# Up projections of m-tiles 2 and 3 as seven block products

## The chip, the cores and the metric

One core of one Trainium2 chip runs the kernel. The metric is the device time of one execution in microseconds (us); three runs of the kernel before took 2712.07 to 2712.29 us, median 2712.2.

## What is computed

A decoder trunk of two layers on one sequence of 512 tokens, 1024 wide, in f32. A layer is a feed-forward half-step (`ffn1`), a mixer with two branches, and a second feed-forward half-step (`ffn2`). Each sub-layer normalizes x and modulates it by a conditioning vector c. Cut to the part that the change touches:

```python
D_MODEL = 1024; SEQ = 512; DEPTH = 2; D_FF = 2816
def swiglu(h, w1, w3, w2):
    return (jax.nn.silu(h @ w1) * (h @ w3)) @ w2
# for each layer:
mod = cond @ ada_w[l] + ada_b[l]
sh1, sc1, g1, sh2, sc2, g2, sh3, sc3, g3 = jnp.split(mod, N_MOD, axis=-1)
h = modulate(x, norm_ffn1[l], sh1, sc1)
x = x + 0.5 * (1.0 + g1)[:, None] * swiglu(h, ffn1_w1[l], ffn1_w3[l], ffn1_w2[l])
...
h = modulate(x, norm_ffn2[l], sh3, sc3)
x = x + 0.5 * (1.0 + g3)[:, None] * swiglu(h, ffn2_w1[l], ffn2_w3[l], ffn2_w2[l])
```

## The kernel before

Activations lie with the feature on the partitions: eight tiles of 128 features by 512 tokens. TensorE (PE) works in a 32-bit format that is short of f32, so every operand is split in a high and a low part: ScalarE (ACT) casts the high part, VectorE (DVE) subtracts it from the value for the low part, and a product is three matmuls: high by high, high by low, low by high (`mm3`, L129). `hhi` and `hlo` are the two parts of h.

A feed-forward's 2816 hidden features are 22 m-tiles of 128. An up projection of one m-tile by w1 or w3 loads a slab of 128x1024 weights (512 KB, `slab`, L115), splits it in two halves of 512 and runs 8 x 3 matmuls of 512 columns. There are two ways in which an m-tile's hidden features come about:

- plain: `first` (L546) does m-tiles 0 and 1 from slabs, three of them loaded and split during the sub-layer before (`early`); `up` (L535) does one more m-tile from two slabs. `glu` (L529) makes silu(p1) * p3 and splits it.
- pairs (`pairs`, L630): two m-tiles at once. The 1024 inputs are halved in two blocks of 512, the two m-tiles are the two block columns, the 512 tokens are halved in two. Of the 2x2 by 2x2 product of blocks, seven products are made instead of eight, with sums of weight blocks and combinations of h's blocks (a scheme of Strassen's kind). One product is 24 matmuls of 256 columns and does w1 and w3 together. The seven weight forms (`weights`, L599) are a11, f1, f1+a11, a12, f3, a12+f2 and a22: f1 and f3 are sums of two blocks made on the way in by a load and an accumulating load that POOL issues (`block_sum`, L577), two are made by DVE, and each form is cast by ACT and subtracted by DVE as one piece of 128x1024 (L604 and L605). h's four combinations (`fast_acts`, L470) are made from f32 copies of h, kept in eight "quarters" in the buffers `c3` and `cv`: DVE subtracts (L496) and makes `minus_sum` (L493), POOL subtracts two (L498), ACT and DVE split each into the buffers `A` (L488, L489). They come in four parts, one for each `next(make)`.

The very first feed-forward starts from `first_begun`, with m-tiles 0 to 5 plain. The other three run `first`, two `up`s (m-tiles 2 and 3), pairs from 4 to 9, the first third of the down projection, pairs 10 to 17, the second third, pairs 18 to 21, and the last third (`close`, L422). `early_sums` starts the two sums of the next pairs ahead. `tick` takes the next entry of a queue of `ada_block`s (L276): each loads 512 KB of conditioning weights in an `L` buffer and is one DVE multiplication with a sum (L281). The gate that the first down projection needs is the first eight entries.

Buffers are rings: `raw` has 2, `whi` and `wlo` 3 each, `L` 5, `A` 2; PSUM has `acc` 3, `sc` 2, `sm` 2, `po` 1. Each engine runs its instructions in a fixed order that was set when the program was built; those wrapped in `ordered` keep their order in the text, the others are placed by the builder's scheduler. SP issues most loads, in one queue; POOL issues the accumulating ones, in its own.

Of the kernel before, what the change touches and what calls it, by code (L numbers as in the profile page):

```python
# [73 lines left out]
class Trunk:  # L74
# [435 lines left out]
    def ffn(self, l, w, gate, finish, early, ahead=None):  # L510
# [6 lines left out]
        def up_slab(src, m):  # L517
            return self.slab(src[l, m].rearrange("p k c -> p (k c)"), 1024)

        def place(m):  # L520
            if m in (8, 9):
                hi, lo = (self.t("c3", [P, SEQ], F32R) for _ in range(2))
            else:
                o = self.t("O", [P, 2, SEQ], F32R)
                hi, lo = o[:, 0, :], o[:, 1, :]
            g[m] = (hi, lo)
            return hi, lo

        def glu(m, ps1, ps3):  # L529
            s = self.t("g", [P, SEQ])  # L530
            nc.scalar.activation(s, ps1, AF.Silu)
            nc.vector.tensor_mul(s, s, ps3)
            self.split(*place(m), s)

        def up(m, make):  # L535
            s1 = up_slab(w1, m)
            s3 = up_slab(w3, m)
            next(make)
            ps1, ps3 = self.p("acc"), self.p("sc")
            self.proj(ps1, s1, acts)  # L540
            self.proj(ps3, s3, acts)
            glu(m, ps1, ps3)
            if m > 1:
                self.tick(2)

        def first():  # L546
            s10, s30, s11 = early
            p10, p30, p11 = self.p("acc"), self.p("sc"), self.p("acc")
            for cols in HALVES:
                for k in range(KT):  # L550
                    for s, p in ((s10, p10), (s30, p30), (s11, p11)):
                        self.proj(p, s, acts, cols, (k,))
            glu(0, p10, p30)
            s31 = self.slab(w3[l, 1].rearrange("p k c -> p (k c)"), 1024,
                            tuple(self.t("O", [P, 1024], F32R) for _ in range(2)))
            p31 = self.p("sc")
            self.proj(p31, s31, acts)
            glu(1, p11, p31)
            return 2

        def first_begun():
            n = len(early) // 2
            s = up_slab(w3, n)
            for m in range(n):
                glu(m, early[2 * m], early[2 * m + 1])
            ps = self.p("sc")
            self.proj(ps, s, acts)
            glu(n, early[2 * n], ps)
            return n + 1
# [12 lines left out]
        def loads(m, sums_first=False):  # L582

            st = {}
            st["f1"] = block_sum(m + 1, 0, m + 1, 1)
            if sums_first:
                st["f3"] = block_sum(m + 1, 0, m, 0)
            yield st
            st["a11"] = block("raw", m, 0)
            yield st  # L590
            if not sums_first:
                st["f3"] = block_sum(m + 1, 0, m, 0)
                yield st
            st["a12"] = block("raw", m, 1)
            yield st
            st["a22"] = block("L", m + 1, 1)
            yield st
# [29 lines left out]
                    self.mm(ps[:, i, :], f[0][:, c], x[1], start=False, stop=False, skip_group_check=True)  # L627
                    self.mm(ps[:, i, :], f[1][:, c], x[0], start=False, stop=k == 3, skip_group_check=True)

        def pairs(ms, comb, lds, make=iter(())):  # L630
            half = lambda tag: self.t(tag, [P, 2, 256])
            bank = lambda tag: self.p(tag, [P, 2, 256])
            stream, steps = [], iter(())
# [14 lines left out]
            for m in ms:  # L648
# [13 lines left out]
                for step in range(7):  # L662
# [36 lines left out]
                    else:  # L699
# [1 line left out]
                        s = self.t("cv", [P, 256])  # L701
                        gated(x, 1, HALVES[0], s)
                        self.split(*place(m + 1), gm[1])
                self.tick(2)

        def early_sums(m):
            lds = loads(m, True)
            next(lds)
            return lds
# [12 lines left out]
                       (0, 0) if i == 2 else (2, 1), 4 if i == 2 else 0)  # L722

        begun = len(early) > 3
        plain = 6 if begun else 4
        m = first_begun() if begun else first()
        comb = []
        make = self.fast_acts(comb)
        lds = early_sums(plain)
        while m < plain:  # L730
            up(m, make)
            m += 1
        pairs(range(plain, 10, 2), comb, lds, make)
        lds = early_sums(10)
        down(0)
        pairs(range(10, 18, 2), comb, lds)
        lds = early_sums(18)
        down(1)
        pairs(range(18, FT, 2), comb, lds)
        down(2)  # L740

# [969 lines left out]
```

## Time and profile before

| | |
|---|---|
| median of three runs | 2712.2 us (2712.07 to 2712.29) |
| the profiled execution's own time | 2711.74 us |
| its span, first to last instruction | 2709.6 us |
| PE busy | 2678.9 us (99%) |
| DVE busy | 1988.0 us (73%) |
| ACT busy | 1283.3 us (47%) |
| POOL busy | 225.8 us (8%) |
| granted TensorE clock | 1.00 |

The span is 2.1 us shorter than the time of its execution. Times below are counted from the span's start. In a row of the order of time stand: start, length, engine, line, operation, out<-in by the program's names, shape, and in brackets how long the engine had been idle and who ended that. In a row of a stretch stand: the stretch, its length, then each engine's busy time and number of instructions, the clock, the DMA share and GB/s. PEld is the weight load beside a matmul. q1 is SP's DMA queue and q0 POOL's.

The second feed-forward of layer 0 has its opening products from 1018.0 to 1036.86, the fourth projection and both `up`s to 1064.64, and three pairs to 1125.12.

### The profile page before, as it was taken

Reading aid. Unit: us, or ns where it says so; the run is one execution under the profiler, and the core shown is the slowest. Engines: PE = TensorE matmul, PEld = TensorE weight load, DVE = VectorE, ACT = ScalarE, POOL = GpSimd, SP = SyncE. Lnnn points to the kernel's source line nnn. Section 1 sums busy time; section 2 is a strip of 40 time slices with the busy share of each in tenths; the row PEclk is TensorE's granted clock in tenths of the full one; section 3 lists DMA queues with packets and bytes.
Section 4 is the critical chain, followed back from the end, with each engine's and each line's share of the span. In section 5 each row is a group of like instructions: output and inputs, shape, how many; then the busy total and the mean of one; then the engine's idle time right before and its main releaser. Section 6 shows DMA issues by size and latency. Waiting matters only on the chain.

```text
span 2709.6 us, 44272 instructions
## 1 busy us (share of the span) xinstructions
PE 2678.9 (99%) x17028; PEld 2380.4 (88%) x17028; DVE 1988.0 (73%) x4129; ACT 1283.3 (47%) x2549; POOL 225.8 (8%) x368
## 2 busy tenths in 40 slices
PE   7999999999999999999999999999999999999999
PEld 6989997888888789999999999888888888998988
DVE  6877868777668777785677877786777687685745
ACT  4535355544446436443554344545444564453533
POOL 0000012000001011000010000120000111110000
PEclk9999999999999999999999999999999999999999
DMA  9678723222122563785528875232222225456642
GB/s 308 183 233 225 230 90 118 90 69 84 64 80 72 170 203 113 241 239 154 154 84 227 244 241 162 95 119 76 82 81 73 73 84 183 156 166 177 168 130 85
DMA packets 119107, 394.64 MB, mean 146 GB/s; under 512 B 13552, under 2 KB 16368, under 8 KB 118896
## 3 DMA queue, kind: packets, MB, share of 16 engines
q1 hardware_dynamic: 106368, 350.39, 39.1%
q0 software_dynamic: 10080, 36.70, 7.6%
q10 hardware_dynamic: 2448, 4.72, 0.5%
q8 instruction: 134, 2.20, 0.3%
q14 instruction: 77, 0.63, 0.1%
HBM read 376.55 MB, written 15.20 MB: 145 GB/s over the span
## 4 chain that ended last, share of the span: by engine, by line
PE 94%; DVE 2%; ACT 2%; DMA 0%; issue 0%; POOL 0%; SPq 0%; ACTq 0%; DVEq 0%
PE acc L95 67%; PE sc L95 18%; PE sm L95 6%; PE sm L100 2%; PE po L95 1%; ACT whi L123 0%; ACT g L1274 0%; DVE wlo L124 0%; PE po L100 0%; DMA M<-in_x 0%; DMA raw<-in_w_in 0%; DVE A L1234 0%; DVE mx L1269 0%; DVE s L1229 0%; ACT hhi L401 0%
## 5 line engine op out<-in xcount | busy, mean ns | idle before, releaser
L123 ACT CAST whi<-raw 128x512 fp32r<-128x512 f32 (+2 forms) x548 | 315.5, 607 | 444.0 <-PE acc L95 216.2
L95 PE MATMUL acc<-hhi,whi 128*128 128x512 f32 (+1 forms) x1368 | 505.5, 370 | 2.3 <-ACT whi L1527 2.3
L95 PE MATMUL acc<-hhi,wlo 128*128 128x512 f32 (+1 forms) x1368 | 487.3, 356 | 0.0
L95 PE MATMUL acc<-hlo,whi 128*128 128x512 f32 (+1 forms) x1368 | 485.4, 355 | 0.0
L124 DVE TENSOR_TENSOR wlo<-raw,whi 128x512 fp32r<-128x512 f32 (+2 forms) x548 | 374.8, 703 | 122.6 <-ACT whi L123 115.6
L95 PE MATMUL acc<-O,whi 128*128 128x512 f32 x1472 | 454.7, 390 | 0.0
L95 PE MATMUL acc<-A,whi 128*128 128x256 f32 (+1 forms) x1808 | 346.5, 291 | 0.3 <-ACT g L684 0.2
L95 PEld LDWEIGHTS acc<-O,whi 128*128 128x128 f32 x1472 | 274.9, 188 | 56.2
L95 PEld LDWEIGHTS acc<-hhi,wlo 128*128 128x128 f32 x1368 | 259.2, 189 | 38.6 <-DVE wlo L124 1.9
L95 PEld LDWEIGHTS acc<-A,whi 128*128 128x128 f32 x1808 | 286.1, 192 | 5.7 <-ACT g L684 0.4
L95 PE MATMUL acc<-O,wlo 128*128 128x512 f32 x736 | 286.8, 390 | 0.0
L95 PEld LDWEIGHTS acc<-hhi,whi 128*128 128x128 f32 x1368 | 259.9, 190 | 30.3 <-ACT whi L1527 2.4
L95 PEld LDWEIGHTS acc<-hlo,whi 128*128 128x128 f32 x1368 | 260.2, 190 | 27.1
L95 PE MATMUL acc<-A,wlo 128*128 128x256 f32 (+1 forms) x904 | 262.6, 291 | 0.0
L604 ACT CAST whi<-L 128x1024 fp32r<-128x1024 f32 x140 | 147.1, 1051 | 202.7 <-issue 75.9
L605 DVE TENSOR_TENSOR wlo<-L,whi 128x1024 fp32r<-128x1024 f32 x140 | 171.2, 1223 | 34.0 <-ACT whi L604 32.9
L95 PEld LDWEIGHTS acc<-A,wlo 128*128 128x128 f32 x904 | 173.3, 192 | 2.5
L605 DVE TENSOR_TENSOR wlo<-raw,whi 128x1024 fp32r<-128x1024 f32 x105 | 128.5, 1224 | 62.1 <-ACT whi L604 60.7
L419 DVE SCALAR_TENSOR_TENSOR M<-acc,gate,M 128x512 f32<-128x512 f32 (+1 forms) x112 | 77.4, 691 | 126.0 <-PE acc L95 125.8
L604 ACT CAST whi<-raw 128x1024 fp32r<-128x1024 f32 x105 | 110.1, 1048 | 121.7 <-PE acc L95 46.8
L95 PEld LDWEIGHTS acc<-O,wlo 128*128 128x128 f32 x736 | 138.2, 188 | 28.7
L281 DVE SCALAR_TENSOR_TENSOR L<-L,kph 128x1024 f32<-128x1024 f32 x126 | 150.2, 1218 | 4.3 <-DMA L<-in_ada_w 4.3
(443 smaller groups left out, 5256.7 us busy)
## 6 DMA issues: line engine op xcount, KB each, us to landing
raw<-in_ffn_w SPq DMA_DIRECT2D x166, 512.0 KB, 4.1
L<-in_ada_w SPq DMA_DIRECT2D x126, 512.0 KB, 5.1
raw<-in_w_in SPq DMA_DIRECT2D x108, 512.0 KB, 3.3
L<-in_ffn_w SPq DMA_DIRECT2D x105, 512.0 KB, 4.5
L<-in_ffn_w POOLq DMA_DIRECT2D x70, 512.0 KB, 8.7
raw<-in_w_branch_a SPq DMA_DIRECT2D x16, 512.0 KB, 3.4
raw<-in_w_branch_b SPq DMA_DIRECT2D x16, 512.0 KB, 4.3
O<-in_ada_w SPq DMA_DIRECT2D x16, 512.0 KB, 4.7
```

Of the source, the lines that this page charges most:

```text
L95: i = self.nc.tensor.matmul(*a, **k)
L100: i = self.nc.tensor.transpose(*a, **k)
L123: both = [nc.scalar.copy(hi[:, s], raw[:, s]), nc.vector.tensor_sub(lo[:, s], raw[:, s], hi[:, s].bitcast(F32))]
L124: nc.vector.tensor_sub(lo[:, s], raw[:, s], hi[:, s].bitcast(F32))]
L281: self.order(self.nc.vector.scalar_tensor_tensor(raw, raw, 1.0, self.condb, ALU.mult, ALU.mult, accum_out=mod[:, o:o + 1]))
L419: self.nc.vector.scalar_tensor_tensor(self.x[:, m, a:b], ps[:, a:b], gate[:, m:m + 1], self.x[:, m, a:b], ALU.mult, ALU.add)
L604: nc.scalar.copy(hi, t)
L605: nc.vector.tensor_sub(lo, t, hi[:].bitcast(F32))
```

## The change

In the three feed-forwards that begin with `first`, m-tiles 2 and 3 are done by `pairs` too, which so starts at 2 instead of 4 (`plain` is 2 and `up` isn't called there). `early_sums(2)` is called ahead of `first`; and the first two parts of the combinations are made in `first`, one behind each `glu`, the other two in steps 0 and 1 of the first pair as before. `ticks` gives the number of ticks behind each pair: 0, 2, 3, 3, instead of 2 behind each `up` and each pair. The first feed-forward keeps its way.

```diff
-        def first():
+        def first(make):
...
             glu(0, p10, p30)
+            next(make)
             s31 = self.slab(w3[l, 1].rearrange("p k c -> p (k c)"), 1024,
                             tuple(self.t("O", [P, 1024], F32R) for _ in range(2)))
             p31 = self.p("sc")
             self.proj(p31, s31, acts)
             glu(1, p11, p31)
+            next(make)
             return 2
...
-        def pairs(ms, comb, lds, make=iter(())):
+        def pairs(ms, comb, lds, make=iter(()), ticks=(2,)):
...
-                self.tick(2)
+                self.tick(ticks[min((m - ms[0]) // 2, len(ticks) - 1)])
...
         begun = len(early) > 3
-        plain = 6 if begun else 4
-        m = first_begun() if begun else first()
         comb = []
         make = self.fast_acts(comb)
-        lds = early_sums(plain)
-        while m < plain:
-            up(m, make)
-            m += 1
-        pairs(range(plain, 10, 2), comb, lds, make)
+        plain = 6 if begun else 2
+        if begun:
+            m = first_begun()
+            lds = early_sums(plain)
+            while m < plain:
+                up(m, make)
+                m += 1
+        else:
+            lds = early_sums(plain)
+            first(make)
+
+        pairs(range(plain, 10, 2), comb, lds, make, (2,) if begun else (0, 2, 3))
```

What the built program makes of it, at three places of the second feed-forward of layer 0. A number behind a name tells one use of a buffer from the next; lines from 554 on stand two to seven further down in the changed kernel (L604 is L606 there).

ACT, from the end of the norm before: `acc_10514` and `acc_10516` are the opening products of w1 (`acc_10520` and `acc_10522` in the change), `raw_10712` is the slab of m-tile 2, `O_10667` the high part of the fourth projection's slab.

```order
L123 CAST whi_10713<-raw_10712 128x512
L531 ACT_TABLE_LOAD
L531 ACTIVATE g_10661<-acc_10514 128x512
L531 ACTIVATE g_10700<-acc_10516 128x512
L123 CAST whi_10713<-raw_10712 128x512
L139 CAST O_10664<-g_10661 128x512
L123 CAST O_10667<-raw_10669 128x512 x2
L123 CAST whi_10721<-raw_10720 128x512 x2
L123 CAST whi_10801<-raw_10800 128x512 x2
L488 CAST A_10728<-c_1820_10401 128x512
L488 CAST A_10728<-c_1821_10408 128x512
```

The same place in the change: `raw_10728` is a11 of m-tiles 2 and 3, `L_10514` is f1, `O_10683` the fourth projection's slab, `A_10673` the first combination and `A_10674` the one that POOL's subtraction goes before.

```order
L606 CAST whi_10734<-raw_10728 128x1024
L531 ACT_TABLE_LOAD
L531 ACTIVATE g_10667<-acc_10520 128x512
L531 ACTIVATE g_10716<-acc_10522 128x512
L606 CAST whi_10738<-L_10514 128x1024
L139 CAST O_10670<-g_10667 128x512
L123 CAST O_10683<-raw_10685 128x512 x2
L677 COPY g_10778<-acc_10753 128x512
L488 CAST A_10673<-c_1820_10401 128x512
L488 CAST A_10674<-c_1829_10475 128x512
L488 CAST A_10673<-c_1821_10408 128x512
```

Weight forms of 1024 stand where halves of 512 stood, the fourth projection's slab comes one whole form later, and the combination's casts have moved up, one of POOL's between them.

PE, at the end of the first product of the new pair (`acc_10753`) in the change: `sc_10691` is the fourth projection and `sc_10793` product two.

```order
L95 MATMUL acc_10753<-hhi_10399,whi_10734 128x256
L95 MATMUL acc_10753<-hlo_10400,whi_10734 128x256
L95 MATMUL acc_10753<-hhi_10399,wlo_10735 128x256
L95 MATMUL sc_10691<-hhi_10399,O_10683 128x512
L95 MATMUL sc_10691<-hlo_10400,O_10683 128x512
L95 MATMUL sc_10793<-A_10673,whi_10738 128x256
L95 MATMUL sc_10691<-hhi_10399,O_10684 128x512
L95 MATMUL sc_10691<-hhi_10399,O_10683 128x512
```

Before, sixteen matmuls of m-tile 2's first projection stood ahead of the fourth projection; now it is the 24 of product one, and a single matmul of product two stands as the third of what follows. `O_10684` is the low part of the fourth projection's slab.

SP and POOL, in the mixer's last projection (`w_out`) ahead of that feed-forward; first SP before:

```order
L574 DMA L_10709<-in_ffn_w 128x1024
L279 DMA L_10794<-in_ada_w 128x1024
L279 DMA L_10797<-in_ada_w 128x1024
L1459 DMA M_9971<-spill 128x512 x8
L120 DMA raw_10135<-in_w_out 128x1024
L279 DMA L_10878<-in_ada_w 128x1024
L120 DMA raw_10141<-in_w_out 128x1024
```

and SP in the change, where `L_10517` is f3 and `L_10732` a22 of m-tiles 2 and 3, `L_10780` and `L_10885` f1 and f3 of m-tiles 4 and 5:

```order
L576 DMA L_10517<-in_ffn_w 128x1024
L576 DMA L_10732<-in_ffn_w 128x1024
L576 DMA L_10780<-in_ffn_w 128x1024
L1466 DMA M_9971<-spill 128x512 x8
L120 DMA raw_10135<-in_w_out 128x1024
L576 DMA L_10885<-in_ffn_w 128x1024
L120 DMA raw_10141<-in_w_out 128x1024
```

POOL in the change, at the same place; before, only the first of the three accumulating loads stood there:

```order
L1459 TENSOR_TENSOR g_9966<-g_9966,M_6484 128x512
L581 DMA L_10517<-in_ffn_w 128x1024
L581 DMA L_10780<-in_ffn_w 128x1024
L581 DMA L_10885<-in_ffn_w 128x1024
L363 TENSOR_TENSOR nv_10350<-nv_10349,power_63 128x2
```

The three places that held ada loads now hold loads of the feed-forward, and two of these have an accumulating load behind them.

## The prediction

> **What bounds the kernel now.** I read the page first, then the chain of waits, then busy time by stretch, then the order of time around one place.
>
> ```profile
> span 2709.6 us, 44272 instructions
> PE 2678.9 (99%) x17028; PEld 2380.4 (88%) x17028; DVE 1988.0 (73%) x4129; ACT 1283.3 (47%) x2549; POOL 225.8 (8%) x368
> PE 94%; DVE 2%; ACT 2%; DMA 0%; issue 0%; POOL 0%; SPq 0%; ACTq 0%; DVEq 0%
> ```
>
> PE sets the end: 94% of the chain is PE. So less PE work gains its own length, if PE is still fed; and every pause of PE is paid in full. The share of 73% for DVE is a mean, so I looked at the stretches that the change replaces. The five below are: the stretch from the end of the three opening products to the first block product in the second feed-forward of layer 0; its first two block pairs; and the first stretch again in layer 1's two feed-forwards.
>
> ```profile
> core 0: us, PE busy (x) PEld busy (x) DVE busy (x) ACT busy (x) POOL busy (x), PEclk, DMA share, GB/s
> 1036.86:1064.64 27.78, 27.78 (x122) 22.47 (x121) 23.27 (x33) 15.34 (x25) 3.39 (x2) 1.00 0.43 133
> 1064.64:1084.80 20.16, 20.16 (x170) 20.15 (x169) 18.52 (x25) 11.61 (x17) 1.77 (x2) 1.00 0.77 215
> 1084.80:1104.96 20.16, 20.16 (x171) 20.16 (x170) 16.86 (x21) 11.30 (x16) 1.71 (x2) 1.00 0.79 220
> 1386.83:1414.44 27.61, 27.61 (x122) 22.53 (x121) 22.81 (x33) 13.88 (x24) 2.94 (x2) 1.00 0.41 134
> 2375.64:2403.44 27.80, 27.80 (x123) 22.48 (x122) 23.47 (x33) 15.35 (x25) 3.38 (x2) 1.00 0.39 133
> ```
>
> PE is never idle here, the clock is 1.00, and DVE is already busy 18.5 of 20.2 us in a block pair.
>
> **PE work.** Matmuls are pipelined, so I take start to start, not the mean of one:
>
> ```profile
> 1036.58 0.28 PE L95 MATMUL acc<-hlo,whi 128*128 128x256 f32 x1
> 1036.70 0.28 PE L95 MATMUL acc<-hhi,wlo 128*128 128x256 f32 x1
> 1036.86 0.50 PE L95 MATMUL acc<-hhi,whi 128*128 128x512 f32 x1
> 1037.19 0.40 PE L95 MATMUL acc<-hlo,whi 128*128 128x512 f32 x1
> 1037.58 0.50 PE L95 MATMUL acc<-hhi,wlo 128*128 128x512 f32 x1
> 1047.19 0.39 PE L95 MATMUL acc<-hlo,whi 128*128 128x512 f32 x1
> 1047.42 0.39 PE L95 MATMUL acc<-hhi,wlo 128*128 128x512 f32 x1
> ```
>
> 0.12 us for 256 columns, 0.227 for 512 (1047.19 to 1047.42). The plain pair is 4 projections of 24: 96 x 0.227 = 21.8 us. The block pair is 7 products of 24: 168 x 0.12 = 20.16, which is the second row's length. PE work falls by 1.6 us per sub-layer. With the fourth opening projection (24 x 0.227 = 5.44) the new stretch is 25.6 us if PE never pauses; today's 27.78 holds 27.2 of work and 0.6 of pauses (1036.86 to 1037.58 shows two of 0.33 to 0.39 instead of 0.227). Gain at best: 27.78 + 27.61 + 27.80 - 3 x 25.6 = **6.4 us**, the lower end.
>
> **Whether PE is fed.** Added per sub-layer: 7 casts and 7 subtractions of 128x1024, two sums, three bank copies, the gating; removed: 16 half casts, 16 half subtractions, two gatings. And the first two combinations must be ready before product two and three, not 27 us later.
>
> ```profile
> 1036.18 0.62 ACT L123 CAST whi<-raw 128x512 fp32r<-128x512 f32 x1 [4.13 <-PE acc L95]
> 1036.82 1.28 ACT L531 ACT_TABLE_LOAD   x1
> 1038.12 1.09 ACT L531 ACTIVATE g<-acc 128x512 f32<-128x512 f32 x2
> 1055.53 1.05 ACT L604 CAST whi<-raw 128x1024 fp32r<-128x1024 f32 x1 [0.32 <-DMA raw<-in_ffn_w]
> 1045.63 0.68 DVE L496 TENSOR_TENSOR c<-c,c 128x512 f32<-128x512 f32 x1
> 1046.23 0.68 DVE L496 TENSOR_TENSOR c<-c,cv 128x512 f32<-128x512 f32 x1
> 1058.36 1.22 DVE L281 SCALAR_TENSOR_TENSOR L<-L,kph 128x1024 f32<-128x1024 f32 x1
> 1059.50 1.22 DVE L281 SCALAR_TENSOR_TENSOR L<-L,kph 128x1024 f32<-128x1024 f32 x1
> 1046.39 1.69 POOL L498 TENSOR_TENSOR c<-cv,c 128x512 f32<-128x512 f32 x1 [13.92 <-DVE c L496]
> ```
>
> The first row is the key: ACT stood 4.13 us until PE let go of a slab's buffer. The three whi/wlo buffers hold the opening slabs, so no slab of the pair can be split before 1036.18, in the change as today. From there I walk the queues in the order that the section on the change shows in part, with these durations (back to back DVE takes 1.14 per 1024 and 0.60 per 512, from the starts; ACT about 0.95 and 0.51), in the frame of this execution:
>
> - Product one needs the 1024-wide cast (to 1037.23) and its subtraction (to 1038.45). Today's halves let the third matmul start at 1037.58. PE waits 0.4 + 1.0.
> - The fourth projection, third today, needs its slab's hi part. ACT does table load (to 1038.4), two Silus (39.4), the second slab (40.4), a split (40.9), then it: PE, done with product one at 1041.1, waits 0.4.
> - Two matmuls later stands one matmul of product two, for which DVE's subtraction of quarters (42.2 to 42.8, behind the second slab's wlo) and ACT's cast (to 43.55) are needed: 1.6. Behind it the projection waits for its lo part (44.1): 0.4, and for the second half of it, behind a combination that waits for POOL: 0.3.
> - Product two ends at 1052.2. Then PE wants one matmul of product three: DVE has the slab sum, glu, a wlo of 1.22 and two of minus_sum first, ACT the cast (to 54.0): 1.6. The next one wants product four's wlo (to 55.1): 1.0.
>
> Sum (before rounding) 6.8 us; the stretch ends at 1036.8 + 25.6 + 6.8 = 1069.2 instead of 1064.64. After that DVE has caught up: the slabs of the next pair are split 2 us before PE asks. The walk has no DVE idle above 0.5 us but during POOL's two subtractions.
>
> ```profile
> 1047.12 1.51 DVE L124 TENSOR_TENSOR wlo<-raw,whi 128x512 fp32r<-128x512 f32 x1 [0.21 <-ACT whi L123]
> 1048.03 1.75 POOL L498 TENSOR_TENSOR cv<-cv,cv 128x512 f32<-128x512 f32 x1
> 1049.14 1.79 DVE L489 TENSOR_TENSOR A<-c,A 128x512 fp32r<-128x512 f32 x2
> 1054.64 1.29 DVE L489 TENSOR_TENSOR A<-c,A 128x512 fp32r<-128x512 f32 x2
> ```
>
> These show a further price: beside POOL's L498 a DVE subtraction took 1.51 instead of 0.69, a pair 1.79 instead of 1.29. Today PE has work for 27 us and does not feel it; in the change L498 runs from 1042.9, beside the lo split that PE waits for. I add 1.0 us. [...]
>
> So a second feed-forward costs 25.6 + 7.8 - 27.8 = +5.6, twice. In the first feed-forward of layer 1 the casts of the first combination stand together ahead of POOL's, and the same walk gives 0.4 + 1.0 + 0.8 + 0.4 + 1.4 + 0.8 = 4.9; with 0.8 for POOL, 25.6 + 5.7 - 27.6 = +3.7. Sum **+14.9 us**. Bounds per sub-layer: -2.1 (no pause) and +7.2 (each of eight hand-overs 0.2 us later than walked).
>
> **The loads that move.** SP and POOL now issue the first pair's sums and two of the next pair's during the sub-layer before (the places of three ada loads); so two more accumulating transfers fall there.
>
> ```profile
> q1 hardware_dynamic: 106368, 350.39, 39.1%
> q0 software_dynamic: 10080, 36.70, 7.6%
> L<-in_ffn_w POOLq DMA_DIRECT2D x70, 512.0 KB, 8.7
> M<-spill SPq DMA_DIRECT2D x16, 256.0 KB, 8.1
> 1001.20 0.48 DVE L419 SCALAR_TENSOR_TENSOR M<-acc,gate,M 128x256 f32<-128x256 f32 x1
> 1008.94 0.43 DVE L336 TENSOR_TENSOR g<-g,g 128x256 f32<-128x256 f32 x1 [0.55 <-ACT g L335]
> 1010.24 0.50 PE L95 MATMUL sm<-ones,g 128*128 128x1 f32 x4
> ```
>
> An accumulating one holds all 16 engines for 0.076 x 2709.6 / 70 = 2.9 us. The engines are full there: M's 256 KB take 8.1 us to land. Slabs that land 3 us later are split 3 us later, and DVE's residual (1001.20) and squares stand behind those splits; the last square ends at 1009.37, 0.9 before PE wants it. Bounds 0 (the slab loads have 3 to 4 us to spare) and 3.5 per close; I take 1 for each mixer's close, being nearer to the slack, and 0.5 for the down projection's: **+2.5**.
>
> At nothing: the ada multiplications that leave (two fewer before the first down projection) and come back as a third in later pairs, since 18.52 + 1.14 is under 20.16; if that cover goes, a pair is 0.5 us longer. POOL's earlier place in its queue: its DMAs wait only for loads issued long before.
>
> **Sum.** 14.9 + 2.5 = +17.4 on the profiled execution's 2711.7 (span 2709.6), which is 0.5 below the median; from 2712.2 it is **2729.5 us**. Less than 0.2%, or 5.4 us, can't be told from no change.
>
> **Rivals.**
> - *The covers hold*: DVE's work up to the last subtraction that the pair needs is 9 x 1.14 + 21 x 0.60 = 22.9 us, under 25.6, so in another order PE would not wait: 2712.2 - 6.4 = 2706. For: that sum. Against: the three buffers, free only at 1036.18, and the order. Chance 0.08.
> - *Only DVE's sum counts* (queues less in lockstep than walked): DVE is done at 1037.2 + 22.9 = 1060.1, one product of 2.88 stands behind it, 1063.0 against 1064.6: -1.6 a sub-layer with no waits, +1 with half of them: 2707 to 2717, middle 2712. Chance 0.11.
> - *The close loses as much as the pair*: accumulating loads hold up the slabs by 3.5 us and the norm with them, in all three: 2729.5 + 8 = 2737.5, decided by whether the squares come after PE's sm matmul. Chance 0.12.
> - That the change doesn't do what it says: the order has 168 block matmuls where 96 stood, so no chance.
>
> Forecast 0.69, with its own range of 2719 to 2735. Slower by over 0.2% takes it and the third rival and a little of the second: 0.83; same 0.09; faster 0.08. The range is 2714 to 2739.
>
> **What will show it.** PE rows: pauses of 0.3 to 2.7 us before sc<-A,whi and acc<-A,whi in the first pair, none in the later pairs; that stretch at 32 to 34 us against 27.8; DVE busy over 85% of it; POOL's L498 overlapping a DVE subtraction of 1.5 us or more. A first pair of 20.16 us without pauses proves me wrong; so does a loss that sits in later pairs or in the down projection.

## The result, and the profile after

The change makes the kernel slower: 2750.9 us median of four executions (2745.2 to 2753.1) against 2712.2, a ratio of 1.0137 with an interval of 1.0125 to 1.0149. I had predicted 2729.5 us and a range up to 2739. The direction was right, the size too small, and the time lies outside the range. The profiled execution took 2745.2 us (span 2742.9), 33.3 us of span more than the one of before; it is also the shortest of the four, with a mean granted clock of 0.998, where 2749.8, 2751.9 and 2753.1 us had 0.996, 0.995 and 0.994.

The page of the changed kernel: the span, the busy times and the first line of the chain of waits.

```profile
span 2742.9 us, 44778 instructions
PE 2687.7 (98%) x17244; PEld 2395.3 (87%) x17244; DVE 2014.8 (73%) x4147; ACT 1297.5 (47%) x2561; POOL 231.1 (8%) x374
PE 89%; DVE 4%; ACT 3%; DMA 2%; issue 1%; POOL 0%; SPq 0%; ACTq 0%; DVEq 0%; POOLq 0%
```

PE's share of the chain falls from 94 to 89%. The shares of the whole say no more. Busy time by stretch does: the new first stretch in the second feed-forward of layer 0, the next pair behind it, and the first stretch in layer 1's two feed-forwards.

```profile
1040.50:1074.88 34.38, 29.04 (x194) 26.15 (x193) 30.24 (x38) 20.43 (x31) 4.25 (x3) 0.95 0.34 102
1074.88:1095.04 20.16, 20.16 (x170) 20.16 (x169) 15.55 (x19) 11.17 (x17) 0.86 (x1) 1.00 0.62 167
1400.75:1433.75 33.00, 28.77 (x194) 26.21 (x193) 30.15 (x38) 19.13 (x30) 4.25 (x3) 0.95 0.37 108
2402.07:2437.35 35.28, 29.11 (x195) 26.40 (x193) 30.60 (x38) 20.51 (x31) 4.26 (x3) 0.95 0.35 99
```

The three stretches are 34.38, 33.00 and 35.28 us long, against 27.78, 27.61 and 27.80. The next pair is 20.16 us without a pause, as before. New is the column behind POOL: the granted clock is 0.95, not 1.00. The same view in pieces of 3.41 us shows where, in the first stretch and in the mixer's close of layer 1:

```profile
1046.89:1050.30 3.41, 1.69 (x7) 1.27 (x8) 3.41 (x3) 1.74 (x4) 3.20 (x2) 1.00 0.00 0
1050.30:1053.71 3.41, 3.41 (x10) 2.67 (x9) 3.41 (x6) 0.45 (x1) 0.00 (x0) 0.50 0.22 50
...
2371.26:2374.67 3.41, 0.76 (x7) 0.80 (x8) 1.87 (x5) 1.25 (x3) 0.00 (x0) 1.00 0.68 228
2374.67:2378.08 3.41, 3.41 (x19) 3.41 (x18) 1.41 (x4) 0.42 (x1) 0.72 (x1) 0.50 0.00 0
```

PE ran at half clock for 3.41 us, after 3.41 us in which it had been idle for half of the time or more. (The busy times of this view run past the next matmul's start. Counted from start to start, PE was idle for 2.1 to 3.2 us of the 3.41 us ahead of each half-clock stretch.) This happens four times in this execution (from 1050.30, 1408.70, 2374.67 and 2422.46) and, from 32.0 us, where the record of the clock begins, to 2708.1 us, never in the profiled execution of before. Worked out from the clock of 0.50, PE does 1.7 us less work in 3.41 us at half clock.

PE's pauses in the first stretch, in the order of time (only the rows that have an idle time):

```profile
1040.92 0.39 PE L95 MATMUL acc<-hhi,whi 128*128 128x256 f32 x1 [0.30 <-ACT whi L606]
...
1042.19 0.39 PE L95 MATMUL acc<-hhi,wlo 128*128 128x256 f32 x1 [0.76 <-DVE wlo L607]
...
1045.29 0.50 PE L95 MATMUL sc<-hhi,O 128*128 128x512 f32 x1 [0.21 <-ACT O L123]
...
1047.37 0.38 PE L95 MATMUL sc<-A,whi 128*128 128x256 f32 x1 [1.35 <-ACT A L488]
1048.99 0.73 PE L95 MATMUL sc<-hhi,O 128*128 128x512 f32 x2 [1.24 <-DVE O L124]
...
1060.23 0.38 PE L95 MATMUL acc<-A,whi 128*128 128x256 f32 x1 [1.34 <-ACT A L488]
```

And the close of the mixer in layer 0: PE's wait for the norm's squares, which before did not exist; DVE's rows ahead of it; and the loads of this close (by kind of load: count, KB each, median us to landing).

```profile
1013.81 0.58 PE L95 MATMUL sm<-ones,g 128*128 128x1 f32 x4 [2.73 <-DVE g L336]
```

```profile
1009.71 1.29 DVE L124 TENSOR_TENSOR wlo<-raw,whi 128x512 fp32r<-128x512 f32 x2 [0.29 <-ACT whi L123]
1010.92 0.48 DVE L419 SCALAR_TENSOR_TENSOR M<-acc,gate,M 128x256 f32<-128x256 f32 x1
...
1013.24 0.42 DVE L336 TENSOR_TENSOR g<-g,g 128x256 f32<-128x256 f32 x1 [0.54 <-ACT g L335]
```

```profile
raw<-in_w_out SPq DMA_DIRECT2D x4, 512.0 KB, 7.6
L<-in_ffn_w POOLq DMA_DIRECT2D x3, 512.0 KB, 9.1
```

The kernel before has one accumulating load in this close, the change three. A `w_out` slab takes 7.6 us to land instead of 5.2, as the same view of the kernel before has it:

```profile
raw<-in_w_out SPq DMA_DIRECT2D x4, 512.0 KB, 5.2
...
L<-in_ffn_w POOLq DMA_DIRECT2D x1, 512.0 KB, 9.1
```

The slabs behind it come later one after the other: `raw` has two buffers, so a slab's load waits until the slab two before it is split. The cast of the first of these slabs is 2.55 us later than before (991.23 against 988.68), that of the fourth 5.10. ACT's row of the fourth, before and then after:

```profile
996.37 1.14 ACT L123 CAST O<-raw 128x512 fp32r<-128x512 f32 x2 [1.35 <-DMA raw<-in_w_out]
...
1001.47 1.14 ACT L123 CAST O<-raw 128x512 fp32r<-128x512 f32 x2 [2.66 <-DMA raw<-in_w_out]
```

The slabs' splits stand ahead of DVE's residual and squares. The last square that PE waits for ends at 1013.66, 4.3 us later than before (1009.37), and PE, whose matmuls ahead of it are 0.7 us later than before, stands 2.73 us.

Where the 33.3 us went, from the lag of each matmul behind its counterpart of before, in us (a "close" is the end of a sub-layer, with the next norm):

| place | lag added | of it half clock | forecast |
|---|---|---|---|
| three first stretches | 6.6 + 5.4 + 7.5 | 3 x 1.7 | 5.6 + 3.7 + 5.6 |
| mixer's close of layer 0, last down projection, mixer's close of layer 1 | 3.0 + 2.4 + 5.3 | 1.7 (layer 1) | 1 + 0.5 + 1 |
| later pairs (at 1246 and 1605), close of the first feed-forward of layer 1 | 1.3 + 1.2 + 0.6 | | 0 |

The start of the kernel adds 0.6, and the end gives 0.6 back. Without half clock the stretches lost 14.4 us, the closes 9.0 and the rest 3.1; half clock took 6.8.

### The profile page after: what moved, and what is told of

It reads as the page before. It is cut to its first block, busy times and chain, and to the rows that moved or that the text cites. A ratio compares the mean times of both kernels' runs of the same rounds, so it can differ in the third digit from the quotient of the medians.

```text
span 2742.9 us, 44778 instructions
## 1 busy us (share of the span) xinstructions
PE 2687.7 (98%) x17244; PEld 2395.3 (87%) x17244; DVE 2014.8 (73%) x4147; ACT 1297.5 (47%) x2561; POOL 231.1 (8%) x374
## 4 chain that ended last, share of the span: by engine, by line
PE 89%; DVE 4%; ACT 3%; DMA 2%; issue 1%; POOL 0%; SPq 0%; ACTq 0%; DVEq 0%; POOLq 0%
PE acc L95 63%; PE sc L95 16%; PE sm L95 6%; PE sm L100 2%; PE po L95 1%; DMA raw<-in_w_out 1%; DVE wlo L124 1%; DMA raw<-in_ffn_w 1%; ACT whi L123 0%; DVE O L124 0%; DMA M<-spill 0%; ACT g L1281 0%; PE po L100 0%; DVE g L336 0%; DVE wlo L607 0%
## 5 line engine op out<-in xcount | busy, mean ns | idle before, releaser
L123 ACT CAST whi<-raw 128x512 fp32r<-128x512 f32 (+2 forms) x524 | 301.5, 607 | 435.0 <-PE acc L95 216.7
L95 PE MATMUL acc<-hhi,wlo 128*128 128x512 f32 (+1 forms) x1344 | 475.9, 354 | 2.3 <-DVE wlo L607 2.3
L124 DVE TENSOR_TENSOR wlo<-raw,whi 128x512 fp32r<-128x512 f32 (+2 forms) x524 | 357.7, 702 | 91.5 <-ACT whi L123 84.8
L95 PE MATMUL acc<-A,whi 128*128 128x256 f32 (+1 forms) x1952 | 375.4, 292 | 5.9 <-ACT A L488 4.3
L95 PEld LDWEIGHTS acc<-A,whi 128*128 128x128 f32 x1952 | 310.0, 193 | 12.2 <-ACT A L488 4.9
L95 PE MATMUL acc<-A,wlo 128*128 128x256 f32 (+1 forms) x976 | 284.1, 291 | 0.0
L606 ACT CAST whi<-L 128x1024 fp32r<-128x1024 f32 x152 | 159.6, 1050 | 212.1 <-issue 82.8
L607 DVE TENSOR_TENSOR wlo<-L,whi 128x1024 fp32r<-128x1024 f32 x152 | 186.0, 1224 | 41.8 <-ACT whi L606 40.8
L95 PEld LDWEIGHTS acc<-A,wlo 128*128 128x128 f32 x976 | 188.1, 193 | 2.5
L606 ACT CAST whi<-raw 128x1024 fp32r<-128x1024 f32 x114 | 119.5, 1048 | 137.4 <-PE acc L95 64.0
L581 POOL DMA_DIRECT2D L<-in_ffn_w x76 | 66.5, 875 | 1161.7 <-DMA L<-in_ffn_w 579.1
```

Source lines behind the costliest of these rows:

```text
L95: i = self.nc.tensor.matmul(*a, **k)
L123: both = [nc.scalar.copy(hi[:, s], raw[:, s]), nc.vector.tensor_sub(lo[:, s], raw[:, s], hi[:, s].bitcast(F32))]
L124: nc.vector.tensor_sub(lo[:, s], raw[:, s], hi[:, s].bitcast(F32))]
L581: nc.gpsimd.dma_start(t, w13[l, m2, half2].rearrange("p w k c -> p (w k c)"), accum_op=ALU.add)
L606: nc.scalar.copy(hi, t)
L607: nc.vector.tensor_sub(lo, t, hi[:].bitcast(F32))
```

## The experiments

Theory: the loss has three causes, the places of the combinations in the queues (pauses in the stretches), the two accumulating loads that moved (closes), and half clock behind pauses that lie close together. The rivals stand with each run. "The ratio" is always that to the kernel before, run beside it.

**The clock by itself.** A kernel that leaves out the whole trunk: bursts of matmuls (`busy`, 512 columns each) with pauses of known length between them (`pause(n, ...)` is a chain of n subtractions of 128x512 on DVE, whose result the next burst reads). It was run once.

```diff
+        for ns, times, between in groups:
+            for _ in range(times):
+                ps = busy(70, w)
+                for i, n in enumerate(ns):
+                    if i:
+                        ps = busy(between, w)
+                    w = pause(n, ps)
```

> This kernel leaves out the whole computation: it is a row of bursts of 512-column matmuls (70 each, some 16 us) with pauses between them, and measures the granted clock by itself. A pause is a chain of n subtractions of 128x512 on DVE that the next burst needs; at 0.6 us each and about 0.3 of hand-overs they should be 0.9, 1.5, 2.1, 2.7 and 3.3 us for n = 1 to 5, each 12 times; then 12 groups of two pauses of 1.5 with five matmuls (1.1 us) between, 12 of three such with thirteen matmuls (3 us) between, and 12 of six pauses of 0.9 with 3 us between. Theory A (idle time adds up inside a window of about 3.4 us, the length of each half-clock stretch in the changed kernel's record): none or next to none behind single pauses of 0.9 and 1.5, a part of those of 2.1 to 3.3, and many of the double ones, whose idle time is 3.0 of 4.1 us. Theory B (only a pause that fills a whole window): none anywhere but perhaps at n = 5. Theory C (the clock has nothing to do with the pauses): half-clock stretches in any group at about the same rate, 4 in 2743 us, as the changed kernel had. Each 3.4 us stretch costs 1.7 us of PE.

Busy time by group of pauses, in the order of the expectation (five single lengths, then two, three and six pauses in a group):

```profile
24.00:230.00 206.00, 196.56 (x853) 159.12 (x853) 8.25 (x12) 0.00 (x0) 0.00 (x0) 1.00 0.00 1
255.00:473.00 218.00, 199.82 (x868) 161.64 (x867) 16.56 (x24) 0.00 (x0) 0.00 (x0) 1.00 0.00 1
500.00:740.00 240.00, 213.12 (x862) 170.77 (x861) 24.85 (x36) 0.00 (x0) 0.00 (x0) 0.94 0.00 0
768.00:1015.00 247.00, 211.40 (x849) 169.84 (x849) 33.17 (x48) 0.00 (x0) 0.00 (x0) 0.92 0.00 0
1045.00:1308.00 263.00, 218.68 (x847) 174.96 (x846) 41.48 (x60) 0.00 (x0) 0.00 (x0) 0.90 0.00 0
1338.00:1590.00 252.00, 215.76 (x915) 170.77 (x914) 33.10 (x48) 0.00 (x0) 0.00 (x0) 0.99 0.00 0
1620.00:1950.00 330.00, 275.67 (x1171) 216.63 (x1171) 49.66 (x72) 0.00 (x0) 0.00 (x0) 1.00 0.00 0
1976.00:2425.00 449.00, 392.77 (x1640) 302.06 (x1640) 49.50 (x72) 0.00 (x0) 0.00 (x0) 1.00 0.00 1
```

The pauses came out as 0.94, 1.67, 2.39, 3.12 and 3.85 us. None of the 12 of 0.94 and of 1.67 was followed by half clock; 9 of 12 of 2.39, 11 of 12 of 3.12 and all of 3.85 were. The half-clock stretches start on a grid of 3.413 us (in the changed kernel, too, each is recorded as 3.412 to 3.413 us long, and the four starts lie 105, 283 and 14 such steps apart); a cell is one step of it. Counted on that grid, each matmul as 0.227 us from its start (cells that were themselves at half clock left out), each cell with PE idle for 1.99 us or less was followed by full clock and each with 2.09 or more by half; from 2.05 to 2.07 both happened. The limit in this run is some 2.06 us, 60% of a cell. Theory A holds; B and C fall. But the double pauses, of which I expected many, gave one of 12: two of 1.67 with 1.3 of work between, so placed on the grid that their cells held at most 2.07 us of idle time, just at the limit.

The traces of the trunk bear the limit out. The same count over all thirteen (before, the change and the eleven variants below; the first 45 us left out, since the record of the clock begins only at 32.0 us in the kernel before), with each shape's own time from start to start (0.120 us for 256 columns): 23 cells have 2.11 us idle or more, and half clock follows each of them; it follows none of the other some 10,000, which have 1.93 or less. The norm's matmuls of one column are counted as idle here. Counted as busy they would put one of the 23 out of line, at 1.77 us (ahead of 2352.73 in the run "All three"); that choice was made with this cell in view.

So whether a pause brings half clock depends on where it falls on the grid: of the single ones of 2.39 us, 9 of 12 did. That fits the spread of the changed kernel's executions over 8 us: their clock goes with their times, from 0.998 at 2745.2 us to 0.994 at 2753.1. Only one of the four has a trace.

**The moved loads.** Two L buffers are held, by a copy of one column on POOL, until the norm's last lo part is there.

```diff
             lds = early_sums(plain)
+            for t in [self.t("L", [P, 1024]) for _ in range(2)]:
+                nc.gpsimd.tensor_copy(t[:, 0:1], self.hlo[:, 7, 511:512].bitcast(F32))
             first(make)
```

> The change, with the two L buffers that the second pair's first sums take held until the norm's last lo part is written, so that these two accumulating loads cannot be issued in the close of the sub-layer before. Theory (the moved loads are the loss in the closes): the pauses before sm<-ones,g in the three closes (2.9, 1.1 and 2.9 us) go, PE's lead over the kernel before at these places goes back from 3.6 + 2.3 + 5.3 us to 0, and the stretches keep their 5 to 7 us each; the time falls by 9.5 to 11 us, from 2750.9 to about 2740. Rival (the closes are late for another reason, DVE's and POOL's own work in another order, and the loads are hidden): within 3 us of 2750.9, with the pauses still there.

2735.5 us (2733.9 to 2740.1), ratio 1.0086 (1.0069 to 1.0103): 15.4 less than the change by the medians, more than expected, and 9.2 between the two profiled executions. The pause in the last down projection's close is gone, those in the mixers' closes are smaller:

```profile
1012.92 0.58 PE L95 MATMUL sm<-ones,g 128*128 128x1 f32 x4 [1.07 <-DVE g L336]
...
2367.50 0.58 PE L95 MATMUL sm<-ones,g 128*128 128x1 f32 x4 [0.82 <-DVE g L336]
```

The lag added in the three closes is 1.7 + 0 + 1.0 us instead of 3.0 + 2.4 + 5.3, 8.0 us less, of which 1.7 are half clock; the stretches keep their pauses. The rest of the 15.4 fits the clock, though not shown cell by cell: its mean is 0.997 to 0.998 in all four executions, against 0.994 to 0.998, and 0.002 of 2743 us is 5.5 us. The rival falls, though 1.7 and 1.0 us are left that the two loads don't explain.

The opposite test came last: nothing of the change, only two such loads more in the kernel before.

```diff
         lds = early_sums(plain)
+        if not begun:
+            block_sum(plain + 3, 0, plain + 3, 1)
+            block_sum(plain + 3, 0, plain + 2, 0)
```

> The kernel before, with nothing of the change but two more accumulating loads into L buffers behind the first pair's sums in the three sub-layers (what they fill is not used), so that the same two transfers fall in the same closes as in the change; the ada loads stand behind them. It asks whether the loads alone make the closes' loss, without the combinations and the block products. Theory: the pauses before sm<-ones,g that the change showed (2.7, 0.9 and 2.8 us) appear in the three closes and cost about what the change lost there, 3.0, 2.4 and 3.6 us, some more where a half-clock stretch follows: 2720 to 2726. The stretch behind, with 27 us of work for PE ahead of the first block product, shows no pause above 0.5 us. Rival (the closes lose because of the other order of DVE's and ACT's work): 2712 to 2715.

2737.2 us, ratio 1.0083 (1.0066 to 1.0099): 24.3 us for two loads at three places. PE's rows in the three closes:

```profile
1016.41 0.98 PE L95 MATMUL sm<-ones,g 128*128 128x1 f32 x4 [3.46 <-DVE g L336]
...
1372.47 4.21 PE L95 MATMUL acc<-O,A 128*128 128x256 f32 x18 [6.54 <-DVE M L419]
...
2374.01 0.98 PE L95 MATMUL sm<-ones,g 128*128 128x1 f32 x4 [2.41 <-DVE g L336]
```

The closes lag by 8.4, 8.6 and 8.1 us in the profile, of which three half-clock stretches of 6.83 us make 10.2 in all; no pause of the stretches behind is above 0.5 us. So the loads are enough by themselves. They cost more than in the change, and more than I expected. Here the ada loads stand behind them in the same close (three of each kind, a `w_out` slab takes 8.7 us); that this makes the difference is likely but not tested.

**The combinations' places.** The first two of h's combinations are made under the three opening products.

```diff
         def first(make):
+            for _ in range(2):
+                next(make)
             s10, s30, s11 = early
...
             glu(0, p10, p30)
-            next(make)
...
             glu(1, p11, p31)
-            next(make)
```

> The change, with the first two of h's combinations made under the three opening products instead of behind them (DVE is busy 0.97 of the last 7.5 us there, from 1033.0 to 1040.5 in the changed kernel). The loads stay moved. Theory (the combinations' queue places, not the weights' three buffers, make most of the pauses): the pauses before sc<-A,whi and acc<-A,whi and of the fourth projection's lo part (1.5 + 1.5 + 1.5 in the second feed-forwards) go, those of 0.5 + 0.9 + 0.4 stay; each of the three stretches is 4 to 5 us shorter, and where the half-clock stretch behind them goes too, another 1.7: the time falls by 12 to 18 us, to 2733 to 2739. Rival (DVE's sum and the three buffers set it): the two slabs of the first products can be split no sooner, so that the pauses move to whi and wlo: less than 5 us gained.

2738.8 us (2738.0 to 2740.8), ratio 1.0096 (1.0081 to 1.0111): 12.1 less by the medians, at the weak end of what I expected. Of the six pauses of the first stretch two are left, both of product one's slab:

```profile
1047.54 0.39 PE L95 MATMUL acc<-hhi,whi 128*128 128x256 f32 x1 [1.99 <-ACT whi L606]
1048.80 0.41 PE L95 MATMUL acc<-hhi,wlo 128*128 128x256 f32 x1 [0.75 <-DVE wlo L607]
```

The waits for A are gone, so the queue places made them. The wait for whi has grown from 0.30 to 1.99, since ACT now casts the combinations ahead of it. The closes still lose; half clock stands in the two mixers' closes and in all three stretches.

**All three.** Both edits, and the fourth projection's slab loaded and split ahead of the gating (`s31 = self.slab(...)` stands ahead of the opening products), so that PE has 5.4 us of work while product one's slab is split. What this third edit brings was not run by itself.

> The change with both edits, and with the fourth opening projection's slab loaded and split ahead of the opening products' gating, so that PE has 5.4 us of work while the first pair's slabs are split. Theory: nothing is left of the losses in the closes (11.2 us) and of the pauses in the stretches (6.6 + 5.4 + 7.5 with the half-clock stretches); what remains is PE's work, 25.6 to 26 us per stretch against 27.7: 2706 to 2709, faster than both kernels. Rivals: the half clock is not bound to the pauses and stays (4 to 8 stretches of 1.7 us): 2713 to 2720. Or the losses in later pairs (1.3 + 1.2) are the change's own: 2709 to 2712.

2712.4 us (2710.8 to 2717.1), ratio 1.0001 (0.9992 to 1.0010): the whole loss of the change is gone, though not as much gained as I expected. The mixer's close of layer 0 and the down projection's lose nothing; layer 1's mixer close still loses 3.3 (1.7 of it half clock), the later pairs 1.1 and 1.8. In each stretch one place is left, ahead of product three's parts, of 0.4 to 1.2 us; the two pauses of product one's slab are gone. DVE's rows under the opening products show what sets the place that is left:

```profile
1031.81 1.78 DVE L496 TENSOR_TENSOR c<-c,cv 128x512 f32<-128x512 f32 x1
1033.51 1.83 DVE L489 TENSOR_TENSOR A<-c,A 128x512 fp32r<-128x512 f32 x2
1035.26 2.39 DVE L493 SCALAR_TENSOR_TENSOR c<-c,cv 128x512 f32<-128x512 f32 x2
1037.58 1.46 DVE L489 TENSOR_TENSOR A<-c,A 128x512 fp32r<-128x512 f32 x2
```

POOL's L498 subtractions run at the same time, and DVE's take up to 1.78 instead of 0.69.

**The tick table.** Ten ada multiplications ahead of the first down projection, as before, instead of eight: with all three edits `(0, 2, 3)` becomes `(2, 2, 3)`, in the change alone `(0, 4, 3)`.

> The kernel with all three edits, and the ada multiplications ahead of the first down projection ten again as in the kernel before (2, 2, 3, 3 behind the four pairs) instead of eight (0, 2, 3, 3). What is left of losses there are pauses of 0.60 us at 1235.45 and 1.23 us at 1585.69 before acc<-A,whi, where ACT had stood 3.0 us for an L slab's DMA. Theory (the two ada loads that the change put off past the down projection, at 1198 and 1202 us, hold up the later pairs' slabs): both pauses go, and the second layer's feed-forward of the same kind loses nothing either: 1 to 2.5 us less, about 2710.5. Rival (it is the order of the loads behind the down projection, whatever is in it): the pauses stay, and the first pair, which has two multiplications of 1.14 us more on DVE, is 0 to 2 us slower: 2712 to 2714.

> The change with one edit: ticks 0, 4, 3, 3 instead of 0, 2, 3, 3, so that ten ada multiplications stand ahead of the first down projection as before. Theory (the put-off ada loads are the loss in the later pairs): the pauses of 0.73 and 1.16 us at 1246 and 1605 go, the rest stays: 2748 to 2750 against 2750.9, and in the trace no step of the lag behind the kernel before between the end of the stretch and the last down projection, where the change lost 1.3 and 1.2 us. Rival: the pauses stay, 2750 to 2752.

2715.9 us (ratio 1.0012, 1.0003 to 1.0021) and 2765.9 us (1.0185, 1.0168 to 1.0203): 3.5 and 15 us *slower* than with eight. Both expectations miss. The pause at 1235 did go, but others came in earlier pairs (0.99 us at 1090, 0.67 at 1111). In the change with ticks of four, ACT stood for 7.5 us for a slab, PE waited for that slab's cast, and half clock followed; this execution has ten half-clock cells instead of four.

```profile
1125.83 0.50 PE L95 MATMUL sc<-A,whi 128*128 128x256 f32 x2 [1.88 <-ACT whi L606]
```

```profile
1124.73 1.04 ACT L606 CAST whi<-L 128x1024 fp32r<-128x1024 f32 x1 [7.49 <-DMA L<-in_ffn_w]
```

So a tick costs more than its 1.14 us on DVE, two of them 3.5 and 15 us in these runs: its load takes one of the five L buffers and 512 KB of the queues, beside the accumulating loads. How the 15 us divide between late slabs and half clock I did not work out. Taking the put-off ada loads back does not take the loss back, so they don't account for it; where the pauses in the later pairs come from stays open.

**POOL's subtraction on DVE, and the sums pinned.** On the kernel with ten ticks: L498 as an ordered subtraction on DVE behind the second combination; or, in place of held buffers, the second pair's accumulating loads kept behind L498 in POOL's queue.

> The same, and the combination that POOL subtracts (L498) made by DVE, behind the second one. In the kernel with all three edits DVE's instructions beside POOL's took 1.78 (one), 1.83 and 2.39 us (two each) instead of 0.69 and 1.29, so that the first slab's hi part came at 1038.2 instead of 1036.9 and PE stood 0.92 + 0.25 us before product three's lo part. [...]

> The kernel with all three edits and ten multiplications, but the second pair's accumulating loads kept behind POOL's subtraction in POOL's queue, in place of the L buffers held: the two plain loads that fill these buffers fall in the close again, only the accumulating halves do not. It tells apart whether the accumulating transfer or any transfer is the loss in the closes. Theory (the accumulating ones): the closes lose no more than with held buffers, 0 to 1.6 us, time within 1.5 us of the kernel with ten multiplications. Rival (any 512 KB load there): the pauses of 1 to 2.9 us before sm<-ones,g are back, 5 to 9 us more.

2713.6 us (1.0002, 0.9993 to 1.0012) and 2716.0 us (1.0011, 1.0001 to 1.0020). The first is 2.3 us below its base, with no pause above 0.3 us in the three stretches; DVE's rows there:

```profile
1031.76 0.68 DVE L496 TENSOR_TENSOR c<-c,cv 128x512 f32<-128x512 f32 x1
1032.93 1.30 DVE L489 TENSOR_TENSOR A<-c,A 128x512 fp32r<-128x512 f32 x2 [0.49 <-ACT A L488]
1034.14 1.29 DVE L493 SCALAR_TENSOR_TENSOR c<-c,cv 128x512 f32<-128x512 f32 x2
```

So POOL's subtraction beside DVE made the pause (1.78, 1.83 and 2.39 us for the same three rows with it), not the amount of DVE's work, which grew. I had expected about 1 us less in each of the two second feed-forwards and 2707 to 2709 us if POOL's subtraction set the pause, and within 1 us of the base if DVE's order did. The gain over the base is the one expected; the time named was not reached, because the base itself came out 5 us above its own. The second equals its base, with no pause before sm<-ones,g in layer 0 and one of 0.56 us in layer 1: plain loads in the close do no harm that shows, the accumulating halves do (a `w_out` slab takes 5.3 us to land, with these halves in the close 7.6).

**The best of both.** Eight ticks again, the subtraction on DVE; with held buffers, with the sums pinned behind the norm's last lo part, and the latter with two ticks behind every pair.

> The kernel with all three edits (L buffers held, ticks 0, 2, 3, 3), and L498's subtraction on DVE. Theory: the subtraction on DVE takes the pause of 0.92 us before product three away as it did beside ten multiplications (stretch of 25.6 to 25.8 us), and without the two early ada loads no pauses come up in the first four pairs: each of the three stretches 0.9 to 1.3 us shorter than with all three edits, 2709 to 2711 in all, faster than both kernels by a hair (0.1%). Rival (what one pause gives back the next load or wait takes): 2712 to 2714, the same as both.

> The same, but the second pair's accumulating loads queued behind the norm's last lo part on POOL, in place of the L buffers held by a copy on POOL. Theory (accumulating loads only): the closes as in the kernel before, 0 to 1 us each; the copies (1.1 us on POOL, beside which DVE's instructions are slow) are gone: 2708 to 2711. Rival (plain 512 KB loads there cost too): 1 to 2 us more in each close than with held buffers, 2712 to 2715.

> The same as the one before with two ada multiplications behind every pair (2, 2, 2, 2: eight, as in the change, but none behind the others three). Theory (a third ada load in a pair crowds the slabs): the losses of 1 to 2 us in the third and fourth pair do not come up, but the two loads ahead of the second pair hold up its first slabs: within 2 us of the one before. Rival (only the loads ahead of the second pair matter): 2 to 5 us slower than with 0, 2, 3, 3.

2711.0 us (0.9993, 0.9984 to 1.0002), 2710.0 (0.9991, 0.9982 to 1.0000) and 2715.6 (1.0010, 1.0001 to 1.0019), against 2713.1 of the kernel before beside them. The second is the fastest I have, by 0.1%, which is too little to be told from no change. Its three stretches:

```profile
1037.40:1063.23 25.83, 25.83 (x195) 24.87 (x194) 23.09 (x30) 17.09 (x25) 0.86 (x1) 1.00 0.51 136
1387.00:1412.61 25.61, 25.61 (x194) 24.65 (x193) 23.72 (x31) 15.79 (x24) 0.94 (x2) 1.00 0.56 148
2375.70:2401.49 25.79, 25.79 (x196) 24.83 (x195) 23.05 (x30) 17.05 (x25) 1.20 (x2) 1.00 0.50 137
```

PE is never idle in them, 77.2 us instead of 83.2: the 6 us that the block products can give are there. Half of them are lost again in other places: pauses of 1.1 and 0.9 us in the later pairs, and smaller ones. In layer 1's close PE's pause before sm<-ones,g is 0.3 us with the sums pinned and 1.7 in the kernel with held buffers; which of these differences belongs to the kernel and which to the execution, I can't tell. Two ticks behind every pair cost 5.5 us against 0, 2, 3, 3: the rival had 2 to 5 us for the loads ahead of the second pair. That it is these loads is inferred from the tick table alone.

## Where the prediction failed, and where it was right

- *PE's work* (25.6 us per stretch without pauses): right; 25.6 to 25.8 us measured once nothing waits.
- *The walk through the queues*: right. Taking 25.6 and one half-clock stretch of 1.7 off the three stretches leaves 7.1, 5.7 and 8.0 us of pauses; I had 7.8, 5.7 and 7.8, the price beside POOL's L498 included (the parts of the 5.7 add up to 5.6). Start to start, the pauses of the first stretch are 0.46 and 0.92 (walked: 0.4 + 1.0), 0.37 (0.4), 1.52 (1.6), 1.50 with 0.36 behind it (0.4, 0.3 and 1.0 for L498), 1.50 (1.6) and 0.41 (1.0). By the third run the places of the combinations made the pauses before A and before the projection's lo part; the three buffers made the first two (ACT stood 4.13 us until PE let go of a slab, as before).
- *The price beside POOL's L498*: right; a subtraction of DVE took 1.76 us beside L498 in the changed kernel, and moving L498 to DVE took away the last pause. The 1.0 us itself (0.8 in layer 1's first feed-forward) was my estimate, which no run shows: the rows of before had 0.82 us more for one subtraction (1.51 instead of 0.69) and 0.50 for a pair, the changed kernel's row has 1.07 (1.76 instead of 0.69). In these rows DVE's subtraction ends at 1048.94, 0.55 us behind POOL's end at 1048.39; in the rows of before it was 1048.63 behind 1048.08.

```profile
1047.18 1.76 DVE L124 TENSOR_TENSOR O<-raw,O 128x512 fp32r<-128x512 f32 x1
...
1046.74 1.65 POOL L498 TENSOR_TENSOR c<-cv,c 128x512 f32<-128x512 f32 x1 [10.63 <-DVE c L496]
```

- *The moved loads*, "I take 1 for each mixer's close, being nearer to the slack, and 0.5 for the down projection's: +2.5": this step failed. The three closes lost 9.0 us without half clock, 6.5 more than forecast. I set the slack (0.9 us at the squares, 3 to 4 at the slabs) against one load that is 3 us late. But the lateness is passed on from slab to slab through two `raw` buffers (2.55 us at the first, 5.10 at the fourth), and behind the splits to residual and squares. That was the mechanism of my third rival, at 3.5 us a close; I gave it 0.12, and it is what happened, with 3.0, 2.4 and 3.6.
- *The clock*: missing. I quoted 1.00 in five rows and took it for a constant, while I predicted pauses of up to 2.7 us close together in a kernel that had none. Half clock took 6.8 us in the profiled execution. The other three, whose clock is lower, are 4.6 to 7.9 us longer. Without half clock the profiled execution would have come to 2738.4 us, still 9 above the forecast but just inside the range.
- *Later pairs "at nothing"*: this failed too, by 3.1 us. I had priced a tick by DVE's cover alone; the tick table shows that its load counts as well, but not that this makes these pauses. The prediction said that a loss in later pairs or in the down projection would prove it wrong, and for these 3.1 + 2.4 us it does.

14.4 + 9.0 + 3.1 + 6.8 = 33.3 us. The forecast had 14.9 + 2.5 + 0 + 0, with the first term right to half a microsecond. The range's upper end took the closes at 3.5 us each but no clock, and lay 12 us below the median.

Open: the pauses in the later pairs; the 1.7 and 1.0 us that the mixers' closes kept with the buffers held; and how the half clock fell in the executions that have no trace.

## What to carry to other kernels

Where a change lets PE pause, add up its idle time by steps of 3.4 us: in these runs 2.1 us or more of it in one step brought half clock in the next, at a price of some 1.7 us, and more often in some executions than in others (mean clock 0.994 to 0.998 in the changed kernel's four). When buffers come free earlier, look where the loads that wait for them will land, and price a late slab by the whole chain behind it to the next norm, accumulating loads first. Work for a stalled stretch can be moved into an engine's idle time just ahead of it: here DVE was idle for 6.5 of 7.5 us under the opening products. Two short edits that use it, and the held loads, brought back all that the change had lost; no more than 0.1% came on top.

## What the runs showed of the hardware

At half clock a matmul of 512 columns took 0.427 us from start to start, against 0.227 (the clock kernel, and the changed kernel from 1050.63 to 1053.62). Half clock came in cells of 3.413 us, on a grid that was fixed within each execution, after a cell in which PE had been idle for more than about 2.05 us (the clock kernel). Single pauses of 2.39 us were enough in 9 cases of 12. In the trunk's traces it followed every cell of 2.11 us or more and none of 1.93 or less. So in these runs pauses that filled 60% of a cell were enough for half clock in the next, also as a sum of several (the cell ahead of 1050.30 in the changed kernel holds 2.11 us of idle time, in more than one pause).

Two accumulating loads of 512 KB each, added to a close of the kernel before, cost 8.1 to 8.6 us of PE's time per close, half clock included. In the mixer's close of layer 0, where the DMA share of the kernel before was already 0.98 from 975 to 990 us, a slab of 512 KB then took 8.7 us to land instead of 5.2; with the second pair's plain loads in the change's places and only their accumulating halves put off it was 5.3.
